# Preparing folded weights in a written order, and spreading modulation dots singly behind loads that GpSimd issues

## The chip, the cores and the metric

The kernel runs on one core of one Trainium2 chip. A core has five engines, each with its own in-order queue: TensorE (PE, matmuls), VectorE (DVE), ScalarE (ACT), GpSimd (POOL) and SyncE (SP, which here mostly issues DMAs). They meet through semaphores. The metric is the device time of one execution in microseconds (us).

## The reference, cut to what matters

A two-layer network on 256 latent tokens and 256 context tokens of width 1024, all in float32. Around each mixer (attention in layer 0, an mLSTM in layer 1) stand two half FFNs with a hidden width of 2816, and every step is modulated by nine rows per layer that come from the conditioning vectors:

```python
def half_ffn(h, shift, scale, gate, w_in, w_out, g, b):
    xm = modulate(h, shift, scale)                   # h * (1 + scale) + shift
    a, u = jnp.split(xm @ w_in, 2, axis=-1)
    y = (jax.nn.silu(a) * u) @ w_out
    return post_norm(h, 0.5 * gate * y, g, b)        # layer_norm(ALPHA * h + delta)

mod_lat = jnp.split((jax.nn.silu(c) @ ada_w[i] + ada_b[i])[:, None, :], N_MOD, axis=-1)
mod_ctx = jnp.split((jax.nn.silu(c_ctx) @ ada_w[i] + ada_b[i])[None, None, :], N_MOD, axis=-1)
```

There are four FFNs. Two of them matter here: the second of layer 0 ("FFN 1") and the first of layer 1 ("FFN 2").

## The kernel before, in words

**Precision.** Each float32 operand is split into a high part (ACT's cast, L212) and a low part (DVE's subtraction, L217), and a product is three matmuls: high by high, high by low, low by high (`mm3`, L229, L232, L233). So every weight chunk of 128 x 1024 costs one ACT and one DVE pass, or four DVE passes of 256 where `fine` is set, before PE can use it. Raw chunks come by DMA from SP (L197) into four buffers; the split chunks lie in seven.

**An FFN.** The 2816 hidden columns are 22 units of 128. An input unit forms two PSUM tiles, a and u, over the eight blocks of the width (L564); `ffn_g` then takes the silu of a on ACT (L539), the product with u on DVE (L540), and splits it into g (`split`, L212 and L217). After a part's units come eight output tiles d (`unit_out`), each a sum over the part's units, which DVE adds into h (L587). FFN 1's parts have 7, 7 and 8 units, FFN 2's 6, 8 and 8. The first four units of the first part, the lead, run for the latent tokens first and then for the context tokens (256 wide each) while the norm before is still under way; later units run on all 512 tokens. The last six output tiles of the last part, the tail of a folded FFN, run by token group, too, with the next norm between them.

**Folded units.** FFN 1's third part and FFN 2's second and third are folded: the product of a 2 x 2 arrangement of blocks (two halves of the width, two halves of the tokens; a and u are the two columns) is formed from seven products in place of eight. `fold_x` (L653) makes the sums of the input: t1, t2 and t4 go into tiles of their own, the third overwrites the first half of the context tokens' input. `fold_w` (L680) makes the sums of a unit's two weight chunks: four DVE additions of 512 (L695 to L698), and the splits. `folded` (L707) then runs the seven products of a unit, 84 matmuls of 128 x 256 (L724), in an order that interleaves two units; between them stand small ACT copies and silus (L735, L738, L741, L744, L751) and DVE additions (L748, L754, L756).

**Modulation dots.** A modulation value is the dot of a row of 1024 weights with the silu of a conditioning vector. 128 of them at once are one DVE instruction (L308, 128 x 1024) on one loaded tile of 512 KB (`ada_load`, SP, L302; two buffers). In FFN 1 a loaded tile serves two vectors, so two dots; in FFN 2 one. Between the pieces of the two FFNs the function `pop` loads a tile and forms its dots at once; the table FOLDPOP says how many tiles after each input unit, output tile and tail tile.

**What sets the order.** The program is written in one order, and the tile scheduler places each instruction on its engine's queue; instructions that are passed to `pin` keep their written order among themselves. Before, the matmuls of the folded units and the dots are pinned; ACT's and DVE's work for the folds is not. Names of buffers in the order's rows (t_ and a number) are the scheduler's.

Of the kernel before, what the change touches and what calls it, by code (L numbers as in the profile page):

```python
# [9 lines left out]
F32 = mybir.dt.float32  # L10
# [23 lines left out]
SH = 16  # L34
# [7 lines left out]
FOLDPOP = {  # L42
    1: {
        "in": {0: 1, 1: 1, 2: 2, 3: 2, 4: 3, 5: 3, 6: 3} | {j: 2 for j in range(7, 14)},
        "out": {0: (1, 1, 1, 1, 1, 1, 1, 1), 1: (0, 0, 0, 0, 1, 1, 1, 0)},
        "tail": {},
    },
    2: {
        "in": {0: 2, 1: 2, 2: 2, 3: 2, 4: 2, 5: 2},
        "out": {0: (0, 0, 0, 0, 0, 0, 0, 0), 1: (2, 2, 2, 2, 2, 2, 1, 1), 2: (2, 2)},  # L50
        "tail": {(0, 0): 1, (0, 1): 1},
    },
}
FOLDX = {0: 0, 2: 1}
# [90 lines left out]
class Keep(Stream):  # L145


    def __init__(self, b, chunks, sh=0, seen=None):
        super().__init__(b, chunks, sh)
        self.all = dict([seen.kept]) if seen else {}  # L150

    def __call__(self, i, w=P):
        c, o = divmod(i * P, 1024)
        if c not in self.all:
            self.all[c] = self.b.chunk(self.chunks[c], self.sh(c))
        h, l = self.all[c]
        return h[:, o : o + w], l[:, o : o + w]


class Body:  # L160
# [44 lines left out]
    def chunk(self, src, sh=0):  # L205
        r = self.raw(src)
# [91 lines left out]
    def ada_load(self, layer, dt):  # L298
# [3 lines left out]
        self.nc.sync.dma_start(r, self.a["ada_w"][layer, dt])  # L302
# [240 lines left out]
    def ffn(self, layer, s, gate, groups, side, start=None):  # L543
# [8 lines left out]
        with self.tc.tile_pool(name=f"ffn{li}", bufs=1) as gp:  # L552
# [6 lines left out]
            def unit_in(j, w, g, steps={}):  # L559
                n = g[1] - g[0]  # L560
                pa, pu = self.mm(), self.mm()
                for k in range(ND):
                    for part, o in ((0, pa), (1, pu)):
                        self.mm3(o[:, :n], w(k * 2 + part), self.x(k, g), k == 0, k == ND - 1)  # L564
                    self.steps(steps.get((j, k), ""))
                self.ffn_g(j, pa, pu, g)

            def unit_out(hf, d, w, g, steps={}):
                y = self.mm()
                part_out(hf, d, w, g, y, range(parts[hf]), steps)  # L570
# [22 lines left out]
            for hf in range(len(parts)):  # L593
                last = hf == len(parts) - 1
                js = list(range(ends[hf] - parts[hf], ends[hf]))[0 if hf else done :]
                if hf == 0 and not start:
                    first = js[:LEAD]
                    ws = {j: Keep(self, [w_in[2 * j + i] for i in range(2)], SH) for j in first}
                    for g in groups:
                        assert len(self.running) == (g == LAT)  # L600
                        for j in first:
                            unit_in(j, ws[j], g, LEADSTEP if g == LAT else {})
                            if fold and g == CTX:
                                call("in", j)
                    for j in () if fold else first:
                        call("in", j)
                    js = js[LEAD:]
                folded = None
                if hf >= folds:
                    self.fine = False  # L610
                    folded = self.folded(js, w_in)
                    js = []
                for j in js:
                    unit_in(j, stream(j), allg)
# [7 lines left out]
                w = (Keep if fold else Stream)(self, [w_out[ends[hf] - parts[hf] + i] for i in range(parts[hf])])  # L622
                body = ND - tail if last else ND
                begun = 0
                if folded:
# [8 lines left out]
                    for d in range(2):  # L634
                        part_out(hf, d, w, allg, ys[d], (n - 1,))
                        sum_out(hf, d, allg, ys[d])
                        call("out", hf, d)
                for d in range(begun, body):
                    unit_out(hf, d, w, allg)
                    call("out", hf, d)  # L640
                    if fold and hf == folds - 1 and d in FOLDX:
                        self.fold_x(2 * FOLDX[d])
                if body < ND:
                    w = Keep(self, w.chunks, SH, w)
                    self.fine = True
                    for g in groups:
                        for d in range(body, ND):
                            unit_out(hf, d, w, g, tailstep)
                            call("tail", int(g == CTX), d - body)
                    self.steps(ENDSTEP)  # L650


    def fold_x(self, k):  # L653

        V, S = self.nc.vector, self.nc.scalar
        if k == 0:
            self.th, self.tl = (self.t([P, 3, ND // 2, TL], F32R, pool=self.gp) for _ in range(2))

        def whole(d, g):
            f = self.tmp().rearrange("p (d f) -> p d f", d=2)  # L660
            h, l = (x[:, d : d + 2, g[0] : g[1]].bitcast(F32) for x in (self.xh, self.xl))
            V.tensor_tensor(out=f, in0=h, in1=l, op=ALU.add)
            return f

        f11, f12, f21, f22 = whole(k, LAT), whole(k, CTX), whole(ND // 2 + k, LAT), whole(ND // 2 + k, CTX)
        V.tensor_tensor(out=f11, in0=f11, in1=f12, op=ALU.subtract)
        V.tensor_tensor(out=f12, in0=f22, in1=f12, op=ALU.subtract)
        V.tensor_tensor(out=f22, in0=f22, in1=f11, op=ALU.add)
        V.tensor_tensor(out=f21, in0=f22, in1=f21, op=ALU.subtract)
        ks = slice(k, k + 2)  # L670
        to = [[x[:, i, ks, :] for x in (self.th, self.tl)] for i in range(3)]
        to3 = [x[:, ks, CTX[0] : CTX[1]] for x in (self.xh, self.xl)]
# [922 lines left out]
```

## Time and profile before

| what | us |
|---|---|
| median of 3 runs (lowest, highest) | 1679.69 (1677.86, 1682.78) |
| the profiled execution, and its span | 1678.48, 1676.4 |
| PE, DVE, ACT, POOL busy | 1617.8, 1387.7, 726.5, 93.5 |
| FFN 1: lead for the context tokens ends; first part's units; its output tiles | 631; to 663; to 702 |
| FFN 1: second part's units; its output tiles; folded part | to 778; to 819; to 902 |
| FFN 2: lead for the context tokens; units 4 and 5; output tiles | 975 to 997; to 1019; to 1052 |
| FFN 2: folded part, output tiles, folded part, then its outputs and tail | to 1131; to 1175; to 1255; to 1335 |

In rows by group, the last field is the engine's idle time right before those instructions, with what ended it after `<-`. In rows by stretch, each engine has its busy time and the count of its instructions; PEld is the loading of weights into PE, which overlaps its matmuls. In timelines a row starts with the start and the length in us. DVEq, SPq are the queues of those engines. The granted TensorE clock was 0.995 of full speed over the span.

### The profile page before, as it was taken

What the parts mean: (1) busy time and instruction counts of PE and PEld (TensorE: products, weight loads), DVE (VectorE), ACT (ScalarE), POOL (GpSimd) and SP (SyncE); (2) the same over time, 40 slices, a digit from 0 to 9 for tenths busy, and PEclk for the clock granted to TensorE, in tenths of its full rate; (3) what the DMA queues carried; (4) which work ended last, traced back from release to release, by engine and by line L of the source; (5) the groups of instructions that cost most, each with busy time, mean ns of one, the idle gap of its engine ahead of it and who ended that gap; (6) DMA issues with size and microseconds to landing.
All of it is one profiled execution on the core that took longest, in us unless ns stands there. A gap on an engine that the chain in (4) does not pass through costs nothing. (4 is left out here: it accounts for less than half of the span.)

```text
span 1676.4 us, 26966 instructions
## 1 busy us (share of the span) xinstructions
PE 1617.8 (97%) x10320; PEld 1459.1 (87%) x10320; DVE 1387.7 (83%) x2971; ACT 726.5 (43%) x1286; POOL 93.5 (6%) x114
## 2 busy tenths in 40 slices
PE   7999999999889999999999999999999999999997
PEld 6888888899888897888899998998999888999986
DVE  5799977649988898978987898888888967997686
ACT  4622222314566353223354352552552646566541
POOL 0000000002331100000000100000001002120000
PEclk9999999999999999999999999999999999999999
DMA  9667765522201337765235253346343332337552
GB/s 352 205 216 240 237 212 190 180 69 86 64 1 56 121 108 237 224 198 176 63 101 164 78 195 119 101 152 207 124 160 114 108 126 76 116 124 252 178 176 75
DMA packets 71921, 250.63 MB, mean 150 GB/s; under 512 B 7920, under 2 KB 10480, under 8 KB 71792
## 3 DMA queue, kind: packets, MB, share of 16 engines
q1 hardware_dynamic: 71072, 248.15, 45.7%
q8 instruction: 81, 1.33, 0.3%
q10 hardware_dynamic: 720, 0.76, 0.1%
q14 instruction: 48, 0.39, 0.1%
HBM read 247.83 MB, written 1.05 MB: 148 GB/s over the span
## 5 line engine op out<-in xcount | busy, mean ns | idle before, releaser
L229 PE MATMUL t<-t,t 128*128 128x256 f32 (+2 forms) x2164 | 710.3, 330 | 12.3 <-ACT t L212 9.2
L232 PE MATMUL t<-t,t 128*128 128x256 f32 (+2 forms) x2164 | 710.7, 329 | 2.0 <-DVE t L493 1.1
L233 PE MATMUL t<-t,t 128*128 128x256 f32 (+2 forms) x2164 | 707.5, 328 | 3.1 <-DVE t L217 3.1
L212 ACT CAST t<-t 128x1024 fp32r<-128x1024 f32 (+2 forms) x523 | 442.2, 869 | 498.6 <-PE t L233 189.6
L217 DVE TENSOR_TENSOR t<-t,t 128x256 fp32r<-128x256 f32 (+2 forms) x871 | 547.8, 664 | 99.7 <-ACT t L212 96.5
L229 PEld LDWEIGHTS t<-t,t 128*128 128x128 f32 x2164 | 406.6, 189 | 52.8 <-ACT t L212 11.9
L232 PEld LDWEIGHTS t<-t,t 128*128 128x128 f32 x2164 | 408.7, 189 | 41.0 <-DVE t L493 2.0
L233 PEld LDWEIGHTS t<-t,t 128*128 128x128 f32 x2164 | 407.6, 189 | 41.2 <-DVE t L217 3.7
L308 DVE SCALAR_TENSOR_TENSOR t<-t,t 128x1024 bf16<-128x1024 f32 x224 | 263.2, 1220 | 11.9 <-DMA t<-in_ada_w 11.6
L724 PE MATMUL t<-t,t 128*128 128x256 f32 x2016 | 235.0, 278 | 8.2 <-ACT t L744 3.7
L724 PEld LDWEIGHTS t<-t,t 128*128 128x128 f32 x2016 | 233.1, 188 | 10.6 <-ACT t L744 4.5
L539 ACT ACTIVATE t<-t 128x256 f32<-128x256 f32 (+1 forms) x69 | 33.2, 487 | 131.3 <-PE t L233 130.1
L435 POOL TENSOR_TENSOR t<-t,t 128x256 f32<-128x256 f32 x30 | 23.3, 777 | 1149.4 <-ACT t L425 1147.9
L540 DVE TENSOR_TENSOR t<-t,t 128x256 f32<-128x256 f32 (+1 forms) x69 | 37.4, 549 | 52.9 <-PE t L233 40.3
L587 DVE SCALAR_TENSOR_TENSOR t<-t,t,t 128x256 f32<-128x256 f32 x128 | 57.3, 477 | 28.3 <-PE t L233 28.2
L900 PE MATMUL t<-t,t 128*128 128x256 f32 (+1 forms) x256 | 79.4, 312 | 0.0
L902 PE MATMUL t<-t,t 128*128 128x256 f32 (+1 forms) x256 | 78.8, 310 | 0.0
L901 PE MATMUL t<-t,t 128*128 128x256 f32 (+1 forms) x256 | 78.6, 309 | 0.0
L1339 PE MATMUL t<-t,t 128*128 128x512 f32 (+1 forms) x248 | 55.9, 378 | 10.5 <-ACT t L292 5.0
L1339 PEld LDWEIGHTS t<-t,t 128*128 128x128 f32 x248 | 47.1, 223 | 18.8 <-ACT t L292 5.0
L842 PE MATMUL t<-t,t 128*128 128x512 f32 x264 | 60.0, 389 | 0.0
L425 ACT ACTIVATE t<-t 128x256 f32<-128x256 f32 x72 | 26.1, 413 | 75.1 <-DVE t L418 75.1
(185 smaller groups left out, 1337.6 us busy)
## 6 DMA issues: line engine op xcount, KB each, us to landing
t<-in_ffn_in SPq DMA_DIRECT2D x168, 512.0 KB, 4.3
t<-in_ada_w SPq DMA_DIRECT2D x139, 512.0 KB, 4.0
t<-in_ffn_out SPq DMA_DIRECT2D x66, 512.0 KB, 4.5
t<-in_ffn_last SPq DMA_DIRECT2D x22, 512.0 KB, 3.6
t<-in_att_in SPq DMA_DIRECT2D x12, 512.0 KB, 3.5
t<-in_att_out SPq DMA_DIRECT2D x8, 512.0 KB, 4.0
t<-in_ml_qk SPq DMA_DIRECT2D x8, 512.0 KB, 3.5
t<-in_ml_v SPq DMA_DIRECT2D x8, 512.0 KB, 4.5
```

The costliest lines, as they stand in the source:

```text
L212: self.behind(self.nc.scalar.copy(h, x))
L217: self.behind(self.nc.vector.tensor_tensor(out=ls, in0=xs, in1=hs.bitcast(F32), op=ALU.subtract))
L229: ins = mm(out, wh, xh, start=first, stop=False)
L232: mm(out, wh, xl, start=False, stop=False)
L233: mm(out, wl, xh, start=False, stop=last)
L308: ins = nc.vector.scalar_tensor_tensor(self.tmp().bitcast(BF16), r, 1.0, self.cb[:, v, :], ALU.mult, ALU.mult, accum_out=to)
L724: self.pin(nc.tensor.matmul(o, p, q, start=first and k == i == 0, stop=k == half - 1 and i == 2, skip_group_check=True))
L842: pin(nc.tensor.matmul(ys[tt][i], gs[g], ws[k][w][:, i * 512 : (i + 1) * 512], start=k == 0 and g == w == 0, stop=k == NF - 1 and g == 1,))
L900: mm(o, self.xh[:, k, c], wh, start=k == 0, stop=False)
L901: mm(o, self.xh[:, k, c], wl, start=False, stop=False)
L902: mm(o, self.xl[:, k, c], wh, start=False, stop=k == ND - 1)
L1339: mm = lambda *k, **kw: pin(nc.tensor.matmul(*k, **kw))
```

## The change

- The preparation of a folded unit's weights is cut into five steps (22's half with two of the sums; 11 and 12; the other two sums; s1 and s3; s2 and s4) of pinned ACT and DVE instructions. The first folded unit's steps are written between the output tiles 5, 6 and 7 of the part before; every later unit's between the products of the unit before. The products' own ACT and DVE work is pinned as well.
- `fold_x` is split: t1, t2 and t4 of the input are made ahead of the last two input units of the part before, the third sum (`fold_x3`) behind its first two output tiles.
- Chunks of the output weights in these FFNs are loaded and split a tile ahead, in a written order.
- The tiles of modulation weights in FFN 1 and FFN 2 (72 of 139) are issued from GpSimd's queue, one tile ahead of the dots that use them. Dots are spread one by one over points inside the units and output tiles: for "lead": (12, 16), 12 dots over 16 points; the first only loads. FFN 1's second output stage, and FFN 2's units 4 and 5, third output stage and tail, have no dots any more.

How many dots fall to each stage, before and after:

| stage | before | after |
|---|---|---|
| FFN 1: lead, units 4 to 6, first output tiles | 12, 18, 16 | 11, 14, 17 |
| FFN 1: second part's units, its output tiles | 28, 6 | 38, 0 |
| FFN 2: lead, units 4 and 5, first output tiles | 8, 4, 0 | 13, 0, 5 |
| FFN 2: second output tiles, third ones and tail | 14, 6 | 14, 0 |

Lines move: L212/L217 become L208/L213 (for folded weights L726/L727), L308 L304, L302 L298, L540 L536, L587 L595, L695 to L698 L728, L724 L791; the copies L735, L738, L744 become L800, L803, L809 and the silus L741, L751 L806, L816; fold_x's L662 to L676 become L689 to L708 (third sum L714).

```diff
-FOLDPOP = {
-    1: {
-        "in": {0: 1, 1: 1, 2: 2, 3: 2, 4: 3, 5: 3, 6: 3} | {j: 2 for j in range(7, 14)},
-        "out": {0: (1, 1, 1, 1, 1, 1, 1, 1), 1: (0, 0, 0, 0, 1, 1, 1, 0)},
...
+DOTS = {
+    1: {"lead": (12, 16), "in0": (14, 12), "out0": (17, 16), "in1": (38, 28)},
+    2: {"lead": (14, 16), "out0": (5, 16), "out1": (14, 12)},
 }
...
-    def ada_load(self, layer, dt):
+    def ada_load(self, layer, dt, eng=None):
...
-        self.nc.sync.dma_start(r, self.a["ada_w"][layer, dt])
+        (eng or self.nc.sync).dma_start(r, self.a["ada_w"][layer, dt])
...
                 for j in js:
-                    unit_in(j, stream(j), allg)
+                    if fold and hf == folds - 1 and j >= ends[hf] - 2:
+                        self.fold_x(2 * (j + 2 - ends[hf]))
+                    unit_in(j, stream(j), allg, name=f"in{hf}")
...
+                    prep = {
+                        ND - 4: (lambda: rs.extend(self.fold_load(nj, w_in)),),
+                        ND - 3: (go,),
+                        ND - 2: (go, go),
+                        ND - 1: (go, go),
+                    }
...
                 for d in range(begun, body):
+                    if fold:
+                        for c in chunks(d):
+                            w(c * 8)
+                        for c in (*chunks(d + 1), *chunks(d + 2)):
+                            w.load(c)
+                        for c in chunks(d + 1):
+                            w(c * 8)
+                    for f in prep.get(d, ()):
+                        f()
                     unit_out(hf, d, w, allg)
...
+        high = lambda p, r: pin(S.copy(p[0], r))
+        low = lambda p, r: pin(V.tensor_tensor(out=p[1], in0=r, in1=p[0].bitcast(F32), op=ALU.subtract))
+        add = lambda o, p, q: pin(V.tensor_tensor(out=o, in0=p, in1=q, op=ALU.add))
...
+            step(now)
+            next(prep)()
+            step(now)
+            step(before)
+            next(prep)()
+            next(prep)()
+            step(before)
+            next(prep)()
+            step(now)
+            next(prep)()
+            step(now)
+            step(before)
+            step(now)
             before = now
...
+            def dot():
+                cur, nxt, v = state
+                if cur is None:
+                    state[0] = ada[0], b.ada_load(*ada.pop(0)[:2], nc.gpsimd)
+                    return
+                if nxt is None and ada:
+                    state[1] = ada[0], b.ada_load(*ada.pop(0)[:2], nc.gpsimd)
+                (layer, dt, vecs), r = cur
+                b.ada_dot(r, layer, dt, vecs[v])
+                state[2] = v + 1
+                if v + 1 == len(vecs):
+                    state[:] = [state[1], None, 0]
+
+            def tick(m, n, points):
+                for _ in range((m + 1) * n // points - m * n // points):
+                    dot()
```

219 lines of the change are left out of this document (128 added, 91 removed).

## The prediction

> **What bounds the kernel now.** I read the page's head and busy shares first, then the busy time of each engine in stretches, then the groups of instructions where TensorE (PE) stood idle, and last the timelines of VectorE (DVE) and ScalarE (ACT) around those places.
>
> ```profile
> span 1676.4 us, 26966 instructions
> PE 1617.8 (97%) x10320; PEld 1459.1 (87%) x10320; DVE 1387.7 (83%) x2971; ACT 726.5 (43%) x1286; POOL 93.5 (6%) x114
> L308 DVE SCALAR_TENSOR_TENSOR t<-t,t 128x1024 bf16<-128x1024 f32 x224 | 263.2, 1220 | 11.9 <-DMA t<-in_ada_w 11.6
> L724 PE MATMUL t<-t,t 128*128 128x256 f32 x2016 | 235.0, 278 | 8.2 <-ACT t L744 3.7
> ```
>
> PE is the bound: 97% busy, and the change neither adds nor drops a matmul. So time can only come from, or go into, the moments in which PE waits. The stretches show how near DVE is to being the bound too (each pair is busy us and instructions):
>
> ```profile
> core 0: us, PE busy (x) PEld busy (x) DVE busy (x) ACT busy (x) POOL busy (x), PEclk, DMA share, GB/s
> 663.00:701.50 38.50, 35.73 (x156) 29.02 (x156) 36.22 (x62) 8.39 (x9) 0.00 (x0) 1.00 0.68 216
> 701.50:778.00 76.50, 76.50 (x339) 63.35 (x338) 60.70 (x98) 21.48 (x26) 0.00 (x0) 1.00 0.65 203
> 819.00:901.60 82.60, 77.51 (x668) 76.45 (x667) 72.16 (x110) 47.52 (x80) 0.00 (x0) 1.00 0.40 128
> 970.00:998.00 28.00, 27.98 (x243) 27.66 (x242) 27.38 (x69) 17.51 (x35) 0.00 (x0) 1.00 0.50 171
> 998.00:1018.00 20.00, 20.00 (x90) 16.56 (x89) 13.94 (x36) 5.74 (x7) 0.00 (x0) 1.00 0.80 286
> 1018.00:1051.60 33.60, 33.60 (x149) 27.80 (x149) 30.56 (x54) 10.32 (x16) 0.00 (x0) 1.00 0.16 49
> 1051.60:1131.00 79.40, 76.95 (x666) 76.09 (x665) 67.03 (x91) 45.24 (x78) 0.00 (x0) 1.00 0.43 133
> ```
>
> The first row is the first output tile stage of FFN 1 (2.8 us lost on PE), the second its second part's input units, the third and last are folded parts (5.1 and 2.4 us lost). In 970 to 998, the lead of FFN 2, DVE has 0.6 us free of 28: whatever is put there makes DVE late. POOL does nothing in any of them.
>
> **Part 1, the folded units.** What PE waited for on the product line, and one such wait on ACT:
>
> ```profile
> L724 PE MATMUL t<-t,t x2004: 276/276/386, 818.9 to 1254.2; 128*128 128x256 f32 x183
>   ACT t L744: 8.2, 8
>   ACT t L212: 5.4, 2
>   ACT t L735: 2.6, 4
>   DVE t L217: 1.7, 2
> ...
> 861.28 19.33 PE L724 MATMUL t<-t,t 128*128 128x256 f32 x168 [1.49 <-ACT t L744]
> ...
> 858.45 2.51 ACT L212 CAST t<-t 128x1024 fp32r<-128x1024 f32 x3 [2.93 <-DVE t L698]
> 860.87 0.36 ACT L744 COPY t<-t 128x256 f32<-128x256 f32 x1
> ```
>
> (The releasers' 17.9 us and 16 times hold PE and its weight loads, which wait together: eight stalls, of which PE's own idle is the 8.2 us of the page's row.) ACT is in-order. The copy L744, for which PE waits, stands behind casts of later units' weights, which wait for DVE's sums (L698). The change fixes that order; on ACT, in the steady fold (L212 are the weights' casts before, L726 after; L744 becomes L809):
>
> ```order
> L741 ACTIVATE t_8002<-t_8001 128x256
> L212 CAST t_8115<-t_8101 128x1024
> L212 CAST t_8118<-t_8103 128x1024
> L212 CAST t_8083<-t_7882 128x512
> L744 COPY t_8003<-t_8000 128x256
> ```
>
> ```order
> L816 ACTIVATE t_7898<-t_7896 128x256
> L726 CAST t_8070<-t_7894 128x1024
> L803 COPY t_8019<-t_8016 128x256
> L726 CAST t_8086<-t_7892 128x1024
> L806 ACTIVATE t_8018<-t_8017 128x256
> L822 CAST t_8115<-t_7898 128x512
> L809 COPY t_8019<-t_8016 128x256
> ```
>
> Three casts in a row stood ahead of the copy; now at most one long cast stands between two of the small copies. The price of the stalls: 8.2 us of idle, plus what the modelled ends hide. A matmul lasts 276 ns in the rows but 168 of them take 19.33 us, 115 ns each, so each stall is 0.16 longer than its idle row says, and a second matmul lags some 0.11 behind it. With eight stalls that is 8.2 + 8 x 0.27 = 10.4 us. Can DVE keep up once the order is fixed? The 84 matmuls of a unit take 84 x 0.115 = 9.7 us; DVE was busy 72.16 us in the fold of eight units, 9.0 each, so yes, by 0.7 us a unit. The first unit's weights (behind ACT t L212: 5.4, two waits that begin FFN 1's fold) are now made in the output tiles before, where DVE loses six dots in FFN 1 and had 3.0 us free of 33.6 in FFN 2. I take **-10.4 us**; bounds -4 (only the L744 stalls) and -11.
>
> **Part 2, the dots around FFN 1's first output stage.** Six dots there were ahead of the last input unit's product on DVE, two of them waiting for their rows:
>
> ```profile
> DVE t L308 <- DMA t<-in_ada_w: 2.0, 2, 1.0
> ...
> PE t L229 <- ACT t L212: 2.2, 1, 2.2
> PE t L232 <- DVE t L217: 0.6, 1, 0.6
> ```
>
> In that stage 18 dots, six behind each unit, become 14 at twelve points, and the heap is gone: 2.2 + 0.6 + 0.4 hidden by the pipeline is 3.2 gained, less 0.6 for one dot that still stands there: **-2.6**. In FFN 2's tail six dots (7 us of DVE) go and a PE wait of this size with them, **-0.7**:
>
> ```profile
> PE t L398 <- DVE t L375: 0.7, 1, 0.7
> ```
>
> Where do they go? FFN 1's second input stage had 28 and takes 38, and the first half of fold_x besides (DVE 60.7 of 76.5 before; about 72 after), so the last two units' products are late by about **+1.0** at the stage's end. And FFN 2's lead, with 8 before, takes 13, the crux.
>
> **Part 3, the lead of FFN 2.** A row there serves one dot, there are two buffers, and a row's load now waits on GpSimd until the dot before last has released its buffer. So two dots cost one landing time L, plus one dot, plus a handoff. DVE's order around unit 5, the last of that part, before (L308 dot, L540 the unit's product, L217 low parts):
>
> ```order
> L308 SCALAR_TENSOR_TENSOR t_9906,t_9899<-t_9904,t_5623 128x1024
> L217 TENSOR_TENSOR t_10212<-t_10210,t_10212 128x256 x2
> L217 TENSOR_TENSOR t_10247<-t_10245,t_10247 128x256 x4
> L540 TENSOR_TENSOR t_9980<-t_9980,t_9913 128x512
> L217 TENSOR_TENSOR t_10286<-t_10282,t_10286 128x1024
> L217 TENSOR_TENSOR t_9979<-t_9980,t_9978 128x512
> L308 SCALAR_TENSOR_TENSOR t_9987,t_9899<-t_9985,t_5623 128x1024
> L308 SCALAR_TENSOR_TENSOR t_9991,t_9899<-t_9989,t_5623 128x1024
> ```
>
> and after (L304 dot, here the 11th to 13th; L536 product, first of unit 3, then of unit 4; L689 to L708 fold_x; unit 5's product is 15 rows further on):
>
> ```order
> L304 SCALAR_TENSOR_TENSOR t_9818,t_9760<-t_9800,t_5623 128x1024
> L304 SCALAR_TENSOR_TENSOR t_9834,t_9760<-t_9816,t_5623 128x1024
> L213 TENSOR_TENSOR t_10216<-t_10181,t_10216 128x256 x3
> L304 SCALAR_TENSOR_TENSOR t_9850,t_9760<-t_9832,t_5623 128x1024
> L536 TENSOR_TENSOR t_9852<-t_9852,t_9787 128x256
> L689 TENSOR_TENSOR t_9859<-t_67,t_68 128x512
> L213 TENSOR_TENSOR t_9575<-t_9852,t_9574 128x256
> L689 TENSOR_TENSOR t_9861<-t_67,t_68 128x512
> L689 TENSOR_TENSOR t_9866<-t_67,t_68 128x512
> L700 TENSOR_TENSOR t_9859<-t_9859,t_9861 128x512
> L689 TENSOR_TENSOR t_9871<-t_67,t_68 128x512
> L703 TENSOR_TENSOR t_9866<-t_9866,t_9859 128x512
> ```
>
> Of twelve dots, two stood between the products of units 4 and 5 and two behind; now all 13 stand ahead of the products of units 3, 4 and 5, and 27 rows lie between the 13th and unit 5's low part, 25 of 512 elements and two of 256. When is that needed, and when does it come?
>
> ```profile
> 983.12 1.22 DVE L308 SCALAR_TENSOR_TENSOR t<-t,t 128x1024 bf16<-128x1024 f32 x1
> 984.26 0.08 DVE L308 DVE_READ_ACCUMULATOR t<-t,t 128x1 f32 x1
> ...
> 991.31 1.76 DVE L217 TENSOR_TENSOR t<-t,t 128x256 fp32r<-128x256 f32 x5
> 992.99 0.42 DVE L540 TENSOR_TENSOR t<-t,t 128x256 f32<-128x256 f32 x1
> ...
> 855.92 0.68 DVE L695 TENSOR_TENSOR t<-t 128x512 f32<-128x512 f32 x1
> 856.53 0.68 DVE L697 TENSOR_TENSOR t<-t,t 128x512 f32<-128x512 f32 x1
> ...
> 1051.72 1.46 PE L724 MATMUL t<-t,t 128*128 128x256 f32 x11
> ```
>
> A 512-element step starts 0.61 after the last (855.92 to 856.53), a 256-element one 0.34 (five in 1.68): 25 x 0.61 + 2 x 0.34 = 15.9 us. PE: FFN 2's first output stage is 144 matmuls of 33.60/149 = 0.2255 us before the fold at 1051.72, so it starts at 1019.2; 32 of its matmuls (units 0 to 4 of two tiles, and two of a third) run before unit 5 is needed, at 1026.4. So the 13th dot must end by 1010.5. DVE reaches the first dot when it did before, 984.26 at its end; twelve dots later is 984.26 + 6 x (L + 1.25), 1.14 for a dot and 0.1 for handoffs (an estimate). The landing of such rows, issued by SP (min/median/max; first FFN 1, then this place):
>
> ```profile
> DMA to landing us min/median/max: 3.4/3.9/4.8
> DMA to landing us min/median/max: 3.5/4.5/6.0
> ```
>
> No DMA is issued by GpSimd in the profile of before, so its L is unknown. Bounds: not under 3.4 (the same transfer, the best of SP's), and 6.0, the worst of SP's, above. I take 4.5, the median at this very place, with two rows in flight as there will be: the dot ends at 1018.8, 8.3 late, **+8.3 us** of PE waiting. At 3.9 it is +4.7, at 5.5 +14.3, at 6.0 +17.3; each tenth of L costs 0.6.
>
> [...]
>
> Elsewhere L matters less. FFN 1's second input stage wants 19 rows (two dots each) in 76.5 us, 4.03 each; with two buffers, and a row's second dot up to 2.7 us behind its first, loads keep up until L = 8.06 - 2.7 = 5.3, and beyond that cost 9.5 us per us of L. Fold 2's start may wait for one last dot, **+0.4**. SP's queue loses 72 issues and gives nothing: its loads wait for buffers. POOL's takes them and stands idle there, but for the norm's adds ahead of FFN 2's lead, past which two rows go: the price of two issues, nothing that PE sees.
>
> **Sum** at L = 4.5: -10.4 - 2.6 - 0.7 + 1.0 + 8.3 + 0.4 = **-4.0 us**. The profiled execution took 1678.48, its span plus 2.1, which is 1.2 below the median 1679.69. So 1674.5 by the profile and about **1676 us** as a median.
>
> **The rivals.** *Rows land as fast from GpSimd as SP's best* (L 3.4 to 4.1): the lead costs 1.7 to 6 in place of 8.3: 1669 to 1673. For it: 3.9 is the median over FFN 1, and the DMA engines stand at 0.50 in the lead. Against: the 4.5 at the place itself.
>
> *The lead's dots wait, and PE behind them* (the slower side): at L = 5.5 the lead costs 14.3 and FFN 1's stage 0.2 x 9.5 = 1.9 more, sum +3.9, 1684; at 6.0 it is +17.3 and 6.7 more, +11.7, 1691. It decides from L = 5.2, where the sum passes zero. For it: SP's own worst is 6.0 here, DVE has no slack, and the rows may come no earlier than two per landing. Against: the two output stages behind leave DVE some time, though none of it lies before unit 5.
>
> [...]
>
> *The fold's stalls only move*: the fixed order holds ACT's copies behind a cast that waits for DVE in some other place, since ACT is in-order and a cast still stands ahead of each; the fold then gains 4 in place of 10.4: 1682.
>
> **How the numbers follow.** Chances: forecast (L 4.2 to 5.1) 0.35, fast rows 0.31, waiting lead 0.24, locked descriptors 0.04, moved stalls 0.06. The range 1667 to 1692 goes from the fast rows' best (less 2 for a lead that hides more than I see) to L = 6.0 and its rounding up; the forecast's own is 1673 to 1681. A change of 0.3%, 5 us, is what a measurement of this kernel tells from none: faster is under 1674.7, which the fast rows and a sixth of the forecast give, 0.36; slower is over 1684.7, 0.28; the rest 0.36.
>
> **What would show it.** In the changed kernel's groups: idle of PE on the product line (now L791) falls from 8.2 to under 2, right for part 1, wrong at 4 or more. Rows on POOL's queue get a landing time: 4.2 to 5.1 is the forecast. The dot's line (L304) has DVE idle for its rows in 984 to 1020, about 10 us, and PE shows one wait of some 8 us for a unit's cast or low part near 1026. If that wait is under 3, part 3 is wrong in its plan, not in L alone; if PE waits in FFN 1's second output stage, the 38 dots are the fault.

## The result: 1.1% slower, and the profile after

| kernel | median us | runs | lowest to highest | profiled execution |
|---|---|---|---|---|
| before | 1681.24 | 6 | 1677.86 to 1684.94 | 1678.48 |
| changed | 1700.45 | 6 | 1696.21 to 1705.65 | 1705.65 |

The ratio is 1.0113, 95% interval 1.009 to 1.0136: 19 us slower, where 1676 with a range of 1667 to 1692 was forecast. The two profiled executions lie 27.1 us apart in span, more than the medians, because the changed kernel's is the slowest of its six runs and that of before is near the fastest of its own. So the traces say where the time went, and the medians how much it is.

The changed kernel's page, the rows that answer to those of before:

```profile
PE 1631.1 (96%) x10320; PEld 1465.8 (86%) x10320; DVE 1399.8 (82%) x2979; ACT 725.1 (43%) x1286; POOL 132.5 (8%) x186
L225 PE MATMUL t<-t,t 128*128 128x256 f32 (+2 forms) x2164 | 714.3, 332 | 24.4 <-ACT t L208 19.6
L304 DVE SCALAR_TENSOR_TENSOR t<-t,t 128x1024 bf16<-128x1024 f32 x224 | 265.4, 1220 | 32.1 <-DMA t<-in_ada_w 31.9
L791 PE MATMUL t<-t,t 128*128 128x256 f32 x2016 | 236.4, 278 | 8.4 <-ACT t L809 6.9
t<-in_ada_w POOLq DMA_DIRECT2D x72, 512.0 KB, 4.0
t<-in_ada_w SPq DMA_DIRECT2D x67, 512.0 KB, 4.1
```

DVE waits 32 us for modulation rows in place of 12. The fold's product line waits as long as before (8.4 against 8.2), now mostly for the copy L809. The plain matmuls' first line waits for ACT's cast L208 19.6 us. And the landing of a row is the same from GpSimd as from SP, 4.0 and 4.1 in the median.

All kernels here have 10,320 matmuls in the same stages, so the difference from before can be laid out by stage: the start of a stage's first and of the next stage's first matmul, in each trace, minus the same in before (us; one profiled execution each):

```
                                     changed  fold   dots   copy   SP     lead   units  mix    mix,   mix,   mix,old mix,
                                              alone  alone  first  issues  8      4-6 6         GpSimd skip   fold    2
FFN 1 units 4-6, output tiles          +5.7   +0.9   +5.3   +4.2   +3.9   +6.0   -3.3   -3.3   -0.6   +0.6   -3.3   -1.8
FFN 1 second part, output tiles        -1.8   -2.9   -2.7   -1.7   -2.2   -2.2   -0.8   -3.1   -2.7   -3.1   -3.1   -3.1
FFN 1 fold                             +0.9   +2.0   +0.2   -1.7   +0.6   +0.6   +0.9   -1.7   -1.7   -1.7   +0.6   -1.7
FFN 1 outputs, tail; FFN 2 lead        +2.1   +0.1   +2.9   +0.8   +0.8   +2.6   +0.6   +0.3   +1.9   +0.2   +0.0   +0.1
FFN 2 units 4-5, output tiles         +13.2   +0.9   +9.6  +10.8   +5.5   +3.2   +9.4   +4.3   +5.9   +0.7   +0.0   +2.1
FFN 2 fold 1                           +1.1   +0.7   +0.9   +0.5   +1.9   +2.7   +1.1   -0.2   +0.1   +5.9   +9.9   -0.0
FFN 2 second output tiles              +2.7   +0.0   +4.0   +1.3   +1.6   +0.3   +0.1   +1.8   +4.4   +0.6   +0.9   +1.1
FFN 2 fold 2                           +2.9   +6.1   -0.9   +0.2   +1.5   +2.2   +2.2   -1.8   -1.8   -0.8   -1.2   -0.8
ahead of these stages                  -0.9   -0.7   -0.5   +0.7   -1.3   -1.1   -0.0   +0.4   -2.1   +0.0   -0.7   +1.6
behind them                            +1.3   +0.8   +1.3   +1.2   +0.8   +1.2   +1.1   +2.0   +1.2   -0.5   -2.3   +3.2
```

The columns behind the first are the experiments below: the fold's order alone, the dots alone, the copy first, SP issuing, eight points for FFN 2's lead, six dots in FFN 1's units 4 to 6, the mix, and the mix with GpSimd issuing, with FFN 2's dots skipping the first points, with the old fold, and with FFN 2's dots placed once more. Two of them that are equal in FFN 1 (mix, and mix with skip) differ by 3.9 us in the first row, so single entries under 4 us of that row are within what one execution varies. In the changed kernel two rows make 18.9 of the 27.1: the two places where input units give way to output tiles in a first part. The three folds are 4.9 slower; with the 3.2 gained at the start of FFN 1's (two waits that fall in the second row) it is 1.7, where 10.4 were to be gained.

**FFN 2's units 4 and 5.** The 13 dots, and PE behind them (first VectorE in time, then stretches):

```profile
987.80 1.22 DVE L304 SCALAR_TENSOR_TENSOR t<-t,t 128x1024 bf16<-128x1024 f32 x1
988.95 0.08 DVE L304 DVE_READ_ACCUMULATOR t<-t,t 128x1 f32 x1
...
1029.35 1.23 DVE L304 SCALAR_TENSOR_TENSOR t<-t,t 128x1024 bf16<-128x1024 f32 x1 [2.17 <-DMA t<-in_ada_w]
```

```profile
core 0: us, PE busy (x) PEld busy (x) DVE busy (x) ACT busy (x) POOL busy (x), PEclk, DMA share, GB/s
666.00:672.40 6.40, 0.60 (x3) 0.18 (x1) 6.24 (x7) 3.11 (x4) 0.54 (x1) 0.94 1.00 361
1028.00:1038.50 10.50, 3.56 (x10) 1.74 (x9) 9.15 (x17) 4.88 (x9) 0.53 (x1) 0.76 0.31 100
1038.50:1043.50 5.00, 5.00 (x13) 3.92 (x12) 5.00 (x9) 1.86 (x4) 0.00 (x0) 0.50 0.00 0
```

Twelve dots after the first take 1030.5 - 988.95 = 41.6 us, 6.9 for two. From 1028.0 to 1038.5 PE makes 10 matmuls, where 46 would fit (10.5/0.2255). Its waits there, in PE's timeline:

```profile
1031.41 0.49 PE L225 MATMUL t<-t,t 128*128 128x512 f32 x1 [2.45 <-ACT t L208]
...
1036.17 0.80 PE L225 MATMUL t<-t,t 128*128 128x512 f32 x1 [3.52 <-ACT t L208]
1037.93 0.80 PE L228 MATMUL t<-t,t 128*128 128x512 f32 x1 [0.96 <-DVE t L213]
```

They are for g and low parts of units 3 and 4, whose products (L536) stand on DVE at 1030.50 and 1034.79, behind the 13th dot, the second behind six steps of `fold_x` as well. Then comes what the forecast did not have: 5 us at a granted clock of 0.50, in which PE is "busy" and makes 13 matmuls where 22 would fit. The same pair stands at 666 in FFN 1: a wait of 6 us, with matmuls at half clock behind it until 678.4.

**The change from input units to output tiles in FFN 1.** The silu L535 of the last unit, on ACT:

```profile
669.11 1.04 ACT L208 CAST t<-t 128x1024 fp32r<-128x1024 f32 x1 [5.34 <-DMA t<-in_ffn_out]
670.06 0.59 ACT L535 ACTIVATE t<-t 128x512 f32<-128x512 f32 x1
```

It stands behind a cast of an output chunk, which waits for its load. That load was issued only when DVE's low part of an earlier chunk had given back the raw buffer, and four dots stand ahead of that low part. VectorE, and SP's queue:

```profile
656.85 1.22 DVE L304 SCALAR_TENSOR_TENSOR t<-t,t 128x1024 bf16<-128x1024 f32 x1
...
662.47 1.22 DVE L304 SCALAR_TENSOR_TENSOR t<-t,t 128x1024 bf16<-128x1024 f32 x1
...
663.61 1.22 DVE L213 TENSOR_TENSOR t<-t,t 128x1024 fp32r<-128x1024 f32 x1
```

```profile
664.89 2.61 SPq L193 DMA_DIRECT2D t<-in_ffn_out  x2
```

DVE starts its next instruction at 664.75, when the low part has ended, and the load goes out 0.14 later.

**The folds.** One unit in the middle of FFN 1's fold, both engines and PE:

```profile
879.56 1.23 DVE L727 TENSOR_TENSOR t<-t,t 128x1024 fp32r<-128x1024 f32 x1
879.74 2.88 PE L791 MATMUL t<-t,t 128*128 128x256 f32 x24
...
880.70 0.42 DVE L819 TENSOR_TENSOR t<-t,t 128x256 f32<-128x256 f32 x1
881.15 0.69 DVE L821 SCALAR_TENSOR_TENSOR t<-t,t 128x512 f32<-128x512 f32 x1
881.93 0.62 ACT L822 CAST t<-t 128x512 fp32r<-128x512 f32 x1 [2.13 <-DVE t L821]
882.46 0.37 ACT L809 COPY t<-t 128x256 f32<-128x256 f32 x1
...
882.88 9.79 PE L791 MATMUL t<-t,t 128*128 128x256 f32 x84 [0.25 <-ACT t L809]
```

The copy L809's product ended at about 879.7, but it is pinned behind L822, the cast of the unit before's g, and that waits for two DVE steps behind a weights' low part. Here PE loses 0.4 us. It does so, by 0.3 to 0.7, at 12 of the 21 places where one folded unit follows another, and by 1.4 at each fold's last one, where output weights stand on DVE too.

### The profile page after: what moved, and what is told of

Its sections match the earlier page's. It is cut to its first block, busy times and chain, and to the rows that moved or that the text cites. A ratio compares the mean times of both kernels' runs of the same rounds, so it can differ in the third digit from the quotient of the medians.

```text
span 1703.5 us, 27004 instructions
## 1 busy us (share of the span) xinstructions
PE 1631.1 (96%) x10320; PEld 1465.8 (86%) x10320; DVE 1399.8 (82%) x2979; ACT 725.1 (43%) x1286; POOL 132.5 (8%) x186
## 5 line engine op out<-in xcount | busy, mean ns | idle before, releaser
L225 PE MATMUL t<-t,t 128*128 128x256 f32 (+2 forms) x2164 | 714.3, 332 | 24.4 <-ACT t L208 19.6
L208 ACT CAST t<-t 128x1024 fp32r<-128x1024 f32 (+2 forms) x403 | 340.9, 867 | 432.9 <-PE t L229 187.6
L213 DVE TENSOR_TENSOR t<-t,t 128x256 fp32r<-128x256 f32 (+2 forms) x751 | 430.1, 609 | 71.8 <-ACT t L208 69.0
L225 PEld LDWEIGHTS t<-t,t 128*128 128x128 f32 x2164 | 409.4, 190 | 67.4 <-ACT t L208 23.9
L228 PEld LDWEIGHTS t<-t,t 128*128 128x128 f32 x2164 | 411.5, 190 | 45.7 <-DVE t L823 2.9
L229 PEld LDWEIGHTS t<-t,t 128*128 128x128 f32 x2164 | 410.4, 190 | 41.5 <-DVE t L213 3.7
L304 DVE SCALAR_TENSOR_TENSOR t<-t,t 128x1024 bf16<-128x1024 f32 x224 | 265.4, 1220 | 32.1 <-DMA t<-in_ada_w 31.9
L791 PE MATMUL t<-t,t 128*128 128x256 f32 x2016 | 236.4, 278 | 8.4 <-ACT t L809 6.9
L791 PEld LDWEIGHTS t<-t,t 128*128 128x128 f32 x2016 | 232.2, 188 | 13.1 <-ACT t L809 10.3
L726 ACT CAST t<-t 128x512 fp32r<-128x512 f32 (+1 forms) x96 | 90.2, 943 | 87.0 <-DVE t L728 61.3
L727 DVE TENSOR_TENSOR t<-t,t 128x512 fp32r<-128x512 f32 (+1 forms) x96 | 103.8, 1087 | 2.8 <-ACT t L726 0.3
L595 DVE SCALAR_TENSOR_TENSOR t<-t,t,t 128x256 f32<-128x256 f32 x128 | 56.8, 478 | 53.0 <-PE t L229 52.8
L535 ACT ACTIVATE t<-t 128x256 f32<-128x256 f32 (+1 forms) x69 | 33.1, 486 | 105.2 <-PE t L229 104.1
L298 POOL DMA_DIRECT2D t<-in_ada_w x72 | 38.7, 537 | 421.6 <-DVE t L304 311.0
L536 DVE TENSOR_TENSOR t<-t,t 128x256 f32<-128x256 f32 (+1 forms) x69 | 37.5, 548 | 32.5 <-PE t L229 26.7
```

What stands on the lines that cost most here:

```text
L208: self.behind(self.nc.scalar.copy(h, x))
L213: self.behind(self.nc.vector.tensor_tensor(out=ls, in0=xs, in1=hs.bitcast(F32), op=ALU.subtract))
L225: ins = mm(out, wh, xh, start=first, stop=False)
L228: mm(out, wh, xl, start=False, stop=False)
L229: mm(out, wl, xh, start=False, stop=last)
L304: ins = nc.vector.scalar_tensor_tensor(self.tmp().bitcast(BF16), r, 1.0, self.cb[:, v, :], ALU.mult, ALU.mult, accum_out=to)
```

## The experiments

**Each part alone.** In the first kernel the change's fold order, `fold_x` and output chunks stay, with the old table, `pop` and SP's loads; in the second the dots of the change are put into the kernel before.

```diff
-            for k, (n, points) in fold.items():          # dots of the change
+            for j, n in fold["in"].items():              # fold alone: those of before
+                s["in", j] = lambda n=n: pop(n)
```

> The change's fold order (weights' steps, fold_x, output chunks) with the dots of before: the old table, loads by SP, two or more dots at once. If the written order of the fold is worth what was forecast, it is 10 us faster than before (1670). If its gain is eaten inside the fold, because the copy L809 stands behind the cast of the unit before it (L822), it is within 4 us of before, PE still waits about 8 us on the product line for L809, and the lead of FFN 2 and the first output stage of FFN 1 cost no more than before.

Measured: 1686.31 us (1680.12 to 1688.85), ratio to before 1.002 (1.0007 to 1.0033). So the fold's written order alone gains nothing; it loses 3 us. PE's idle time on the product line is 11.9 us, 6.0 of it for the copy, where about 8 were expected for it. At the start of FFN 1's fold the two waits of 2.6 and 0.8 become 1.0 and 0.4 (the -2.9 in the second row). Both stages of units and outputs cost 0.9 each, as expected of the second theory; what was not expected is fold 2's 6.1. There the dots of before stand in the same tiles as the steps that now prepare the first folded unit's weights, and wait for rows ahead of them (VectorE, then PE):

```profile
1175.14 1.22 DVE L312 SCALAR_TENSOR_TENSOR t<-t,t 128x1024 bf16<-128x1024 f32 x1 [0.76 <-DMA t<-in_ada_w]
...
1176.29 2.36 DVE L738 TENSOR_TENSOR t<-t,t 128x1024 fp32r<-128x1024 f32 x2
```

```profile
1184.54 44.38 PE L802 MATMUL t<-t,t 128*128 128x256 f32 x372 [3.07 <-ACT t L814]
```

Behind this wait the granted clock is 0.50 for 3.4 us.

> The new dots (GpSimd's loads, the new table) in the kernel before, whose fold is left as it was. If the dots alone cost the time, it is 15 to 25 us slower than before: 6 at the end of FFN 1's first input units, 13 around FFN 2's lead. If they cost only together with the written order of fold_x and the output chunks, it is within 5 us of before.

Measured: 1697.17 us (1691.09 to 1698.33), ratio 1.0072 (1.0049 to 1.0096). The dots alone make most of the loss: 12 us by the ratios (8 to 16), under the 15 to 25 that were expected, of the changed kernel's 19. In the trace it is 5.3 and 9.6 us at the two places, with fold_x and the output chunks in their old positions. In FFN 1 it is the same wait, though the chunks' written order isn't there:

```profile
669.09 1.04 ACT L204 CAST t<-t 128x1024 fp32r<-128x1024 f32 x1 [5.63 <-DMA t<-in_ffn_out]
670.04 0.59 ACT L531 ACTIVATE t<-t 128x512 f32<-128x512 f32 x1
```

Six casts of output chunks stand ahead of that silu here and in the changed kernel, four in the kernel before and in the one with the fold's order alone. So two of them moved ahead with the dots, by the scheduler's placing, and not with the written order of the chunks. With the fold's order of before, its three stages take what they took (+0.2, +0.9, -0.9), and the gain at FFN 1's fold start (row 2, -2.7) comes here as well. The fold's product line:

```profile
L725 PE MATMUL t<-t,t 128*128 128x256 f32 x2016 | 236.5, 279 | 3.8 <-ACT t L736 2.0
```

Its idle is 3.8 against 8.2 of before, without a change in the fold. So the gain at the fold's start comes when the six dots leave the tiles before it, under the old order, and most of it comes under the written order with the dots in place. It is one gain, and there only once.

**The copy ahead of the cast.** g's cast becomes a step of its own, run after the next unit's copy.

```diff
             pin(V.scalar_tensor_tensor(sl, u, -1.0, sl, ALU.mult, ALU.mult))
+            yield
             pin(S.copy(gh, sl))
...
             step(before)
             step(now)
+            step(before)
             before = now
```

> The changed kernel with one thing moved: a folded unit's g is cast (L822 of the changed kernel) after the next unit's copy L809, not ahead of it. If PE waits for that copy because the cast ahead of it waits for VectorE, the waits of 0.3 to 1.4 us in each folded unit go, and it is 9 to 11 us faster than the changed kernel (1690). If the copy is late for another reason (ScalarE busy with weights), it gains under 3.

Measured: 1690.39 us (1688.69 to 1698.21), ratio to before 1.0061 (1.0036 to 1.0085), against the changed kernel's 1.0113. Its product line, L792 there:

```profile
L792 PE MATMUL t<-t,t 128*128 128x256 f32 x2016 | 236.5, 279 | 2.6 <-ACT t L801 2.3
```

Idle falls from 8.4 to 2.6 and the wait for the copy is all but gone; the three fold stages fall by 2.6, 0.6 and 2.7, the output tiles after fold 1 by 1.4. That is 7 of the 9 to 11 that were expected, and the ratios' difference of 0.5% (8.7 us, with about 6 either way from the two intervals) fits both. The cause is shown, its size a little under.

**Who issues.**

```diff
-                    state[1] = ada[0], b.ada_load(*ada.pop(0)[:2], nc.gpsimd)
+                    state[1] = ada[0], b.ada_load(*ada.pop(0)[:2])
```

> The changed kernel with the modulation rows issued by SyncE again, dots at the same places. If two buffers and one dot for a row set the pace of FFN 2's lead (two dots per landing, whoever issues), the lead still costs 8 us or more over before and the whole is at most 5 us faster than the changed kernel. If GpSimd's issue or its landing is the cause, the lead's 13 us go and it is about 1686 or less.

Measured: 1689.15 us (1686.27 to 1691.44), ratio 1.0041 (1.0024 to 1.0058), against 1.0113: neither theory. The lead's price falls from 13.2 to 5.5, so issuing matters, and two fifths stay. The landings in the lead, GpSimd's (989 to 1031) and then SP's:

```profile
DMA to landing us min/median/max: 3.7/4.8/7.7
```

```profile
DMA to landing us min/median/max: 3.4/4.4/6.1
```

and the step from a dot's end to the next issue, in GpSimd's queue (the dot ended at 988.95) and in SP's (984.26):

```profile
989.43 0.58 POOL L298 DMA_DIRECT2D t<-in_ada_w  x1 [25.94 <-DVE t L304]
```

```profile
984.38 1.47 SPq L298 DMA_DIRECT2D t<-in_ada_w  x2
```

0.48 against 0.12, and 0.4 in the median landing: with six rows in a chain, 6 x 0.76 = 4.6 of the 7.7, an estimate. Matmuls at half clock for 2.9 us in place of 5.0 are 1 more; some 2 us are left over.

**Fewer dots at the two places**, GpSimd still issuing.

```diff
-    2: {"lead": (14, 16), "out0": (5, 16), "out1": (14, 12)},
+    2: {"lead": (8, 16), "out0": (11, 16), "out1": (14, 12)},
```

> The changed kernel with one number changed: six of the dots of FFN 2's lead go to its first output stage (8 points' worth there in place of 14, 11 in place of 5), GpSimd still issuing. If the lead's 13 us come from 13 dots at two per landing ahead of unit 5's product, seven dots end some 20 us sooner, the wait goes with the half-speed matmuls behind it, and it is 10 to 13 us faster than the changed kernel (1688 to 1690). If GpSimd's rows disturb SyncE's weight loads there, whatever their number, it gains under 5.

Measured: 1696.11 us (1693.71 to 1697.92), ratio 1.0089 (1.0064 to 1.0114): 4 us by the ratios, 10 at the place by the trace (13.2 to 3.2). The two spans are 11.3 apart, but the changed kernel's profiled execution stands 5.2 above its median and this one's (1694.32) 1.8 below, which leaves 4.3. By the medians this is under 5, the sign of the second theory (GpSimd's rows disturb SP's weight loads, whatever their number); against it stands the place itself, which got rid of 10 us with GpSimd still issuing. So the lead's dots are the main cause at the lead; how much of the 10 a median run loses there, the traces of single executions don't tell.

```diff
-    1: {"lead": (12, 16), "in0": (14, 12), "out0": (17, 16), "in1": (38, 28)},
+    1: {"lead": (12, 16), "in0": (6, 12), "out0": (17, 16), "in1": (38, 28), "out1": (8, 16)},
```

> The changed kernel with eight dots moved from FFN 1's units 4 to 6 to the output stage of its second part (6 and 8 in place of 14 and 0). If dots ahead of the last unit's product cause the 6 us wait between input units and output tiles, 4 to 6 us go there; the eight dots in the second output stage may cost up to 3 us at the fold's start (that is what their leaving gained), so 2 to 5 us faster in all. If the wait comes from the output weights' casts, written ahead of the unit's silu on ScalarE and waiting for a load, it stays at 4 us or more.

Measured: 1692.89 us (1689.52 to 1696.27), ratio 1.0078 (1.0048 to 1.0108): 6 us, a little over the 2 to 5 expected. In its stretch 663 to 701.5, the one in which before lost 2.8 us and the changed kernel 5.8, PE is busy throughout:

```profile
663.00:701.50 38.50, 38.50 (x172) 31.90 (x171) 31.95 (x53) 8.19 (x10) 3.71 (x7) 1.00 0.59 194
```

The six casts ahead of the silu are still there; the last of them no longer waits for its load. So the dots are the cause, by way of the raw buffers, and the eight that moved cost nothing at the fold's start.

**All together.** SP issues, the copy goes first, and dots are moved.

```diff
+    1: {"lead": (14, 16), "in0": (8, 12), "out0": (18, 16), "in1": (33, 28), "out1": (8, 16)},
+    2: {"lead": (7, 16), "in0": (4, 8), "out0": (10, 16), "out1": (12, 12)},
```

> Everything that gained so far together: SyncE issues, the copy goes ahead of the cast, FFN 2's lead keeps 6 dots (4 in units 4 and 5, 10 in the first output stage, 12 in the second), FFN 1's units 4 to 6 keep 8, 8 go to its second output stage. If the three causes are separate (lead, fold copy, issuing engine), the gains add up: 1674 to 1679, 2 to 7 us under before. If moving the dots only moves the wait, it is at 1683 or above.

Measured: 1675.36 us (1673.07 to 1678.53, 10 runs), ratio to before 0.9965 (0.9951 to 0.9978). That is 25 us under the changed kernel and 6 under before, as expected if the causes are separate. They are not wholly so: the four gains above, taken singly, are 31 by the ratios. SP's issue and fewer dots shorten the same chain in FFN 2's lead, which may be why; that wasn't tested.

**The mix, with one thing turned back**, first the issuing engine.

> The mixed kernel (copy first, dots moved) with one thing turned back: GpSimd issues the rows again. If GpSimd's issue costs by itself (0.4 us more from a dot's end to the next issue, and two issues ahead of the norm's adds before FFN 2), it is 3 to 8 us slower than the mixed kernel: 2 in FFN 1's tail, the rest in FFN 2's lead and second output stage. If it cost only where 13 dots stood in a row, it is within 2 us of it.

Measured: 1682.04 us (1678.33 to 1686.63, 12 runs), ratio 1.0003 (0.9989 to 1.0018). GpSimd's issue costs 0.38%, 6.4 us, with every dot placed as in the mix. By the trace it is FFN 1's first stage (2.7, within what that row varies), its tail (1.6), FFN 2's lead (1.6) and second output tiles (2.6). The part that a wait shows is the dots' wait for rows, 6.9 us from FFN 2's lead to its second output tiles, against 3.2 under SP; in the second output tiles alone it is 4.0 against 2.0 (the waits there in us, times, longest; GpSimd's, then SP's):

```profile
DVE t L304 <- DMA t<-in_ada_w: 4.0, 3, 2.5
```

```profile
DVE t L304 <- DMA t<-in_ada_w: 2.0, 2, 1.1
```

In the tail and in the second output tiles the granted clock besides is 0.50 for 3.4 us each (from 954.0 and from 1145.2), 1.7 us of work, and in the mix at neither place. So the 6.4 are measured, and how they come about is shown only in part.

Then the fold: the mix's dots and issues in the kernel before, with its unordered fold.

> The mixed kernel's dots (SyncE's loads, moved dots) in the kernel before, with its fold and fold_x as they were. If the written order of the fold, its copy put first, is worth something beside the moved dots, this is 3 to 6 us slower than the mixed kernel (1675), so 1678 to 1681. If the mixed kernel's gain came only from dots leaving the tiles ahead of the folds, it is within 1.5 us of it.

Measured: 1683.78 us (1679.07 to 1687.35, 12 runs), ratio 1.0006 (0.9995 to 1.0017), so 0.4%, 7 us, over the mix. That is over the 3 to 6 expected. In the trace, whose execution stands 4.7 under its median, FFN 2's first fold takes 10.1 more than in the mix, most of it in one wait at its start for weights that ACT and DVE prepare among the output tiles' dots, while the stage ahead of it takes 4.3 less:

```profile
1053.06 0.80 PE L725 MATMUL t<-t,t 128*128 128x256 f32 x2 [6.40 <-ACT t L204]
```

The written order is worth something, then: it lets dots stand in the tiles ahead of a fold. By itself, with the dots as they were, it gained nothing.

**Where FFN 2's dots can stand.** `tick` gets a number of points to leave out at a stage's start.

```diff
-    2: {"lead": (7, 16), "in0": (4, 8), "out0": (10, 16), "out1": (12, 12)},
+    2: {"lead": (10, 16), "out0": (12, 12, 4), "out1": (11, 9, 3)},       # skip
+    2: {"lead": (9, 16), "in0": (2, 8), "out0": (10, 14, 2), "out1": (12, 10, 2)},   # mix 2
```

> The mixed kernel with FFN 2's dots placed anew: 9 in the lead, none in units 4 and 5, 12 in the first output stage from its third tile on, 11 in the second from its later tiles. If the 4 us left at FFN 2's first output stage come from dots that the scheduler puts ahead of unit 5's product, they fall under 2 and it is 2 to 4 us faster than the mixed kernel (1671 to 1673). If they come from fold_x and the output chunks' low parts, which stand there whatever the dots, it stays within 1.5 us.

Measured: 1678.33 us (1677.61 to 1679.93, 7 runs), ratio 0.9975 (0.9963 to 0.9986). The place falls from 4.3 to 0.7, as the first theory has it, and 5.9 us appear at the fold behind it: the weights' steps are now behind the dots. The wait has moved, and the whole is no faster than the mix (1.7 us slower by the ratios, whose intervals overlap).

> The mixed kernel with FFN 2's dots halfway between its two placings: 8 in the lead, 2 in units 4 and 5, 10 in the first output stage from its second tile on, 12 in the second from its third. If the wait is moved, not removed, by where dots stand (VectorE has no free time in FFN 2's units 4 and 5 and first output stage together), it is within 2 us of the mixed kernel. If there is a place where they fit, it is 3 to 5 us faster (1670 to 1672).

Measured: 1675.15 us (1672.73 to 1678.92, 6 runs), ratio 0.9953 (0.9938 to 0.9969), within the intervals of the mix. In the two FFN 2 stages it has 2.1 in place of 4.3 - 0.2. These two are the best versions, some 6 to 8 us under before.

## Why the prediction was wrong

**Part 1, the folded units (-10.4): wrong in its step.** The step said that with the fixed order "at most one long cast stands between two of the small copies", and counted casts. It didn't ask what that one cast waits for. L822 needs two DVE steps that need PE's last product of the unit before; with a weights' low part ahead of them the chain ends some 0.4 us too late at 12 units, and 1.4 too late at each fold's end. The rival "the fold's stalls only move", given 0.06 and a gain of 4, was the right one; the gain was 3.2 at one fold start against 4.9 lost inside the three. And of the old 8.2 on the product line more than half needed no new order: 3.8 were left when only the dots were moved, under the old one.

**Part 2, the dots around FFN 1's first output stage (-2.6): wrong.** It counted dots at the place, 18 down to 14, and called the heap gone. The step took a dot's cost as the place that it takes on DVE's queue ahead of the last unit's product. What it left out is the raw buffers: they come back only when DVE has made a chunk's low part, so four dots ahead of that low part delay a load, the load a cast, and the cast the last unit's silu, which stands behind it on ACT. +5.7 in place of -2.6. That two more such casts stand ahead of the silu came with the dots, not with the chunks' written order, for the dots alone have both the casts and the wait. The +1.0 for the 38 dots of the second input stage was right: -1.8 in the second row is 1.4 beside the 3.2 that the fold's start gained, and PE's one wait in these stages is 1.0, for a cast.

**Part 3, the lead (+8.3 at L = 4.5): the mechanism was right, two terms were too small.** The pace was to be L + 1.25 for two dots, 5.75. It was 6.9: the handoff, an estimate of 0.1, is 0.48 in GpSimd's queue, and the landing, 4.5, was 4.8 in the median and up to 7.7 where output weights shared the DMA engines (busy 0.90 from 1007 to 1015). So the 13th dot ended at 1030.5, not 1018.8: 7.1 of it by the pace, and 4.7 because the first dot ended at 988.95, not at 984.26. The waits on PE, 8.5 us from 1028 to 1038 (2.6, 3.7 and 1.5 by the starts of its matmuls, and 0.6 in two short ones) and 1.7 at 1003.6, are near the forecast's 8.3, but not for its reason alone. The output tiles began later too, at about 1027 in place of 1019.2: 6.0 from the stages ahead of units 4 and 5, and the 1.7. And the forecast followed only unit 5. Its low part began 13.9 us after the 13th dot, at 1044.41, where the forecast had it end 15.9 after; PE lost 0.2 us to it. PE stood still for units 3 and 4, whose products also lie behind the 13th dot, and behind those waits unit 5 was in time. What failed besides is the sum's form: a wait was priced at its length. Behind it 12 matmuls took 0.2 us each more at a granted clock of 0.50 (0.43 in place of 0.226), 2.4 us, and behind FFN 1's wait 11, 2.2 us: 4.6 us that no step held.

**The other terms.** "POOL's takes them and stands idle there ... nothing that PE sees" is not borne out: turning GpSimd's issue back costs 6 us even in the mix. The landing time was what the prediction named as the one unknown, and its median over all loads turned out the same as SP's (4.0 and 4.1; in the lead 4.8 against 4.4); more of the cost came by another way, the handoff. The wait in FFN 2's second output tiles (2.7 where 0.4 was forecast) is the same mechanism as the lead, dots waiting for rows ahead of the last folded unit's low part. The 0.04 for "locked descriptors" was the author's estimate for issues from GpSimd that wait while VectorE runs an instruction: no run here shows such a wait or excludes it, and a median landing of 4.0 on POOL beside 4.1 on SP speaks against one at every issue.

**The range.** 1667 to 1692 took its upper end from L = 6.0 with the fold's 10.4 still credited. With part 1 at zero, the rival at L = 5.5 would have stood at 1694, and with the 4.6 of half speed at 1699. By terms, forecast and trace (us; the trace of the profiled execution, whose sum is 27.2):

| term | forecast | measured |
|---|---|---|
| folded units (three folds, and the -3.2 ahead of FFN 1's) | -10.4 | +1.7 |
| FFN 1, first output tiles | -2.6 | +5.7 |
| FFN 1, second part's 38 dots | +1.0 | +1.4 |
| FFN 1's outputs and tail | 0 | +2.1 |
| FFN 2's lead | +8.3 | +13.2 |
| FFN 2's second output tiles | +0.4 | +2.7 |
| FFN 2's tail and what follows | -0.7 | +1.3 |
| ahead of FFN 1's units | 0 | -0.9 |

The 2.1 at FFN 1's tail, which no step held, goes with the clock. Of all the kernels here four have 1.9 or more in that row, and just these four have a granted clock of 0.50 for 3.4 us there (the changed kernel from 965.1, the others from 954.0 to 965.6), which is 1.7 us of work. All four issue from GpSimd, but two others that do so have neither (0.8 and 0.6).

## What to carry to other kernels

Price an order on a queue by what the instruction ahead waits for, two engines back, and not by how many stand ahead: here one cast ahead of the copy L809, late behind two DVE steps, cost PE 0.3 to 0.7 us at 12 of 21 places. A load that may be issued only when its buffer's last reader is done makes a chain: time its whole round (reader's end, issue, landing, reader; 6.9 us for two dots in FFN 2's lead, where 5.75 was forecast), and put no more such rounds ahead of a product than the time to its use holds. And look at what follows a stall on PE: behind the two long waits here, of 6 and of 8.5 us, the matmuls at a granted clock of 0.50 took 2.2 and 2.4 us more.

## What the runs showed of the hardware that was not expected

**Half clock behind a wait.** Behind the two long waits the granted clock was 0.50, and a matmul of 512 took 0.43 us in place of 0.226. In the mix waits of 1.6 and 0.9 us were enough; waits of 2.8 and 0.9 in the kernel before, at the start of its first fold, were not. The rows below are cut where the clock changes, or one such stretch long. First the changed kernel, then the mix, then before:

```profile
668.20:671.62 3.42, 0.00 (x0) 0.00 (x0) 3.26 (x6) 2.34 (x3) 0.54 (x1) 1.00 1.02 339
671.62:678.44 6.82, 6.00 (x13) 4.42 (x14) 6.82 (x13) 1.81 (x3) 0.53 (x1) 0.50 0.75 268
965.10:968.51 3.41, 3.41 (x18) 3.41 (x18) 3.25 (x16) 0.00 (x0) 0.00 (x0) 0.50 0.35 121
1033.40:1043.64 10.24, 6.51 (x14) 4.76 (x15) 10.24 (x18) 5.03 (x9) 0.00 (x0) 0.50 0.08 31
```

```profile
1014.20:1017.61 3.41, 1.29 (x6) 0.51 (x4) 3.41 (x7) 0.62 (x1) 0.00 (x0) 1.00 0.77 219
1017.61:1021.02 3.41, 3.41 (x8) 2.74 (x9) 3.41 (x7) 0.62 (x1) 0.00 (x0) 0.50 0.47 111
```

```profile
818.97:822.38 3.41, 1.53 (x13) 1.32 (x11) 3.41 (x7) 0.72 (x2) 0.00 (x0) 1.00 0.00 0
822.38:825.80 3.42, 1.93 (x14) 1.73 (x15) 3.39 (x9) 2.57 (x3) 0.00 (x0) 1.00 0.25 22
```

The half clock lasts one, two or three times 3.41 us, and within one trace its stretches begin a whole number of 3.41 us apart (from 671.6 to 965.1 it is 86 of them, to 1033.4 106). A wait's length alone does not decide it, as these rows show: the 3.41 us ahead of the mix's stretch, with PE busy for 1.3 of them, were followed by the half clock; the two stretches of before, in which PE was busy for 1.5 and 1.9, were not. At 965 it came with less waiting than that, 1.06 us, ahead of eight matmuls of one column (L394); what decides it no run here shows. The granted clock also goes with how far the times of one kernel spread: the changed kernel's longest run, 1705.65, has a mean granted clock of 0.988 and its shortest, 1696.21, one of 0.992, and 0.4% of 1700, an estimate of what that costs, is 6.8 of the 9.4 us between them.

**GpSimd's issue.** An issue takes 0.53 us of POOL in the median, and the one at 989.43 comes 0.48 after the dot that it waits for, against 0.33 on SP and 0.12 for its issue at 984.38; the transfer then lands about as soon as SP's does (in FFN 1 3.6 at the least and 3.8 in the median, against 3.4 and 3.9 in the kernel before).
